# Spreading the mLSTM's stabiliser rows from POOL's queue, with the mask and the exponentials placed later

## The chip, the core and the metric

The kernel runs on one core of one Trainium2 chip. A core has TensorE (PE: matrix products and transposes into PSUM; PEld are its weight loads), VectorE (DVE), ScalarE (ACT: copies, activations), GpSimd (POOL: element-wise work in SBUF) and SyncE (SP), which in this kernel only issues transfers between HBM and SBUF. Sixteen DMA engines carry the transfers. Each engine runs its own program in order; where one needs another's result it waits on a semaphore. The metric is the device time of one execution in microseconds; less is better.

## What is computed

One layer of a decoder trunk over 2048 positions of width 1024, in float32: modulation and RMS norm, one combined projection, three mixers beside each other (forgetting attention, an mLSTM with matrix memory, a gated spatial unit), an output projection with residual, and a convolutional feed-forward part with residual. The change lies in the mLSTM. The reference, for one of its chunks:

```python
bcum = jnp.cumsum(fb, axis=-1)
log_d = bcum[..., :, None] - bcum[..., None, :] + ib[..., None, :]
log_d = jnp.where(causal, log_d, -jnp.inf)
log_inter = bcum + m[..., None]
m_t = jnp.maximum(log_inter, jnp.max(log_d, axis=-1))
w_intra = jnp.exp(log_d - m_t[..., None])
...
sc = jnp.einsum('bhtd,bhsd->bhts', qb, kb) * w_intra
num = (w_inter[..., None] * jnp.einsum('bhtd,bhde->bhte', qb, C)
       + jnp.einsum('bhts,bhse->bhte', sc, vb))
h_out = num / jnp.maximum(jnp.abs(den), jnp.exp(-m_t))[..., None]
```

The kernel takes chunks of 128 positions instead of 64; the result is the same. It holds w_intra transposed (keys in partitions, queries along the row), as exp(a_s + ne_t + mask): a_s is a column per head (`acol`), ne_t a row per head that every partition needs, and the mask is 0 or -1e30.

## The kernel before

**The stages.** The combined projection runs first, with attention after it, then the output projection, then the feed-forward part. The projection goes through the positions in two halves of 1024, and in each half through twelve blocks of up to 272 columns of W_in (lines 936 to 947). A block in natural order (`natural`, line 583) computes eight tiles `acc` of 128 positions, each of 24 matmuls (three float32r products over eight blocks of rows, `mm3`). `acc` has three PSUM buffers. What a block does with a tile differs: the blocks of k and q (`use_qk`, line 691) square it on ACT (`ev`, line 694), sum on DVE, take the inverse root on POOL (`ss`, the power instruction in `rsqrt`, line 132) and multiply on DVE (`qn`, line 700), which frees the tile; some steps later the tile is transposed (`turn`, line 703), evicted by ACT and DVE (`qhi`, `qlo`) and written to HBM. Blocks of v are evicted by ACT and DVE (`vhl`); the blocks of the spatial unit use ACT's Gelu (`ev`, line 640, `su`, line 658) and POOL (line 646 and the power instruction of `mu`).

**The mLSTM beside it.** `mlstm(qi)` (line 769) is a generator for 512 positions, four chunks of 128. Two of them are put into `background` behind block 3 of each half (line 982). After a tile's matmuls, `tick` (line 578) advances the first generator by one step, four times out of seven. A step is what lies between two yields.

- The first step computes the scans on DVE and writes `ne`, four rows of 512, to `ne_d` in HBM (line 799).
- Two yields later the columns (`ecol`, `acol`, `dcol`) are made and q, k, v are loaded (lines 803 to 826).
- `raw(n)` (line 830) transposes the keys of chunk n (PSUM tag `mp`, one buffer, also used by `spatial`, line 662, and by the modulation, line 461), copies them to `kT` on ACT (line 836), loads `M1` (line 838) and adds the mask to it on POOL (line 839). The load reads four rows of 128 values and spreads them over 128 partitions: 256 KB in pieces of 512 bytes. `M1` has two buffers.
- `decay(n)` (line 842) takes the four exponentials on ACT in place.
- Chunk n has two steps. In the first, scores and inter-chunk products go into PSUM; DVE multiplies the scores by M1 (`sc`, line 868), which is the last use of that M1, and makes `tm`. `decay(n+1)` is behind that. In the second step come the products with v, `H`, the weighted keys `kw` on POOL (line 884), the state update on DVE (line 898), and `raw(n+2)`.

**What sets the order.** Every transfer is issued by SP, with `dma = nc.sync.dma_start`. The source does not fix the order of an engine's program: a scheduler of the framework places each instruction by when it expects the inputs, a free buffer and the engine; source order ranks what is ready together. Once it is placed, an engine's program is run in order. The framework adds the waits; a transfer into a buffer waits on the issuing engine for the last reader.

Of the kernel before, what the change touches and what calls it, by code (L numbers as in the profile page):

```python
# [8 lines left out]
F32 = mybir.dt.float32  # L9
# [3 lines left out]
ALU = mybir.AluOpType  # L13
# [4 lines left out]
P = 128  # L18
# [15 lines left out]
def trunk(  # L34
# [7 lines left out]
    V, A, G, T = nc.vector, nc.scalar, nc.gpsimd, nc.tensor  # L42
    dma = nc.sync.dma_start
# [3 lines left out]
    def bc(ap, axis, n):  # L47
        u = ap.unsqueeze(axis)
        shape = list(u.shape)
        shape[axis] = n  # L50
        return u.broadcast_to(shape)
# [14 lines left out]
    ne_d = dr.tile([4, S], F32, name="ne_d")  # L66
# [62 lines left out]
    pool, pp = Mem(), Mem(PSUM)  # L129
# [219 lines left out]
    def down_open_right():  # L349
# [14 lines left out]
        ("R", 2048, 1), ("mprev", 20, 2), ("decr", 16, 2), ("ecol", 1088, 2), ("acol", 64, 2), ("dcol", 32, 2),  # L364
        ("qT", 4096, 1), ("kn", 4096, 1), ("v1", 4160, 1), ("H", 4160, 1), ("kT", 1024, 2), ("M1", 2048, 2),
        ("sc", 2048, 2), ("tm", 1040, 1), ("kw", 1024, 2), ("den", 64, 2), ("nd", 64, 2), ("mss", 64, 2),
# [12 lines left out]
    def misc_ps():  # L379
        return pp.tile([P, 512], F32, name="mp", tag="mp")  # L380

    def mps():
        return pp.tile([P, 512], F32, name="mps", tag="mps")
# [365 lines left out]
    maskT = pool.tile([P, P], F32, name="maskT")  # L749
# [19 lines left out]
    def mlstm(qi):  # L769
        t0 = qi * 512  # L770
# [56 lines left out]

        got = {}

        def raw(n):  # L830

            kps = misc_ps()
            for j in range(2):
                T.transpose(kps[:, j * P : (j + 1) * P], kn[:, n, j * P : (j + 1) * P], ident)
            kT = pool.tile([P, 2, P], F32, name="kT", tag="kT")
            A.copy(kT.rearrange("p a b -> p (a b)"), kps[:, 0:256])
            M1 = pool.tile([P, 4, P], F32, name="M1", tag="M1")
            dma(M1, ne_d[:, t0 + n * P : t0 + n * P + P].unsqueeze(0).broadcast_to([P, 4, P]))
            G.tensor_tensor(M1, M1, bc(maskT, 1, 4), op=ALU.add)
            got[n] = kT, M1  # L840

        def decay(n):
            M1 = got[n][1]
            for h in range(4):
                A.activation(M1[:, h, :], M1[:, h, :], AF.Exp, bias=acol[:, n, h : h + 1])

        yield
        raw(0)
        yield
        decay(0)  # L850
        raw(1)
        yield
        for n in range(4):
            ch = slice(n * P, n * P + P)
            kT, M1 = got.pop(n)

            sc = pool.tile([P, 4, P], F32, name="sc", tag="sc")
            tm = pool.tile([P, 4, 65], F32, name="tm", tag="tm")
            for par in range(2):
                hp = slice(par * 64, par * 64 + 64)  # L860
                eo = mps()
                for j in range(2):
                    T.matmul(eo[:, j * P : (j + 1) * P], kT[hp, j, :], qT[hp, j, ch], start=True, stop=True)
                for j in range(2):
                    T.matmul(
                        eo[:, 256 + j * 65 : 321 + j * 65], qT[hp, j, ch], Cst[hp, j, :], start=True, stop=True
                    )
                V.tensor_tensor(
                    sc[:, par::2, :], eo[:, 0:256].rearrange("p (j t) -> p j t", j=2), M1[:, par::2, :], op=ALU.mult
                )  # L870
                V.tensor_tensor(
                    tm[:, par::2, :], eo[:, 256:386].rearrange("p (j e) -> p j e", j=2),
                    bc(ecol[:, n, par:4:2], 2, 65), op=ALU.mult,
                )
            if n < 3:
                decay(n + 1)
            yield
            nps = mps()
            for h in range(4):
                T.matmul(nps[:, h * 65 : h * 65 + 65], sc[:, h, :], v1[:, n, h, :], start=True, stop=True)  # L880
            V.tensor_tensor(H[:, n], nps[:, 0:260].rearrange("p (h e) -> p h e", h=4), tm, op=ALU.add)

            kw = pool.tile([P, 4, 64], F32, name="kw", tag="kw")
            G.tensor_tensor(
                kw, kn[:, n, :].rearrange("p (h d) -> p h d", h=4), bc(ecol[:, n, 64:68], 2, 64), op=ALU.mult
            )
            ups = mps()
            for pr in range(2):
                T.matmul(
                    ups[:, pr * 130 : pr * 130 + 130],  # L890
                    kw[:, 2 * pr : 2 * pr + 2, :].rearrange("p h d -> p (h d)"),
                    v1[:, n, 2 * pr : 2 * pr + 2, :].rearrange("p h e -> p (h e)"),
                    start=True, stop=True,
                )
            for h in range(4):
                pr, hf = h // 2, h % 2
                hp = slice(hf * 64, hf * 64 + 64)
                V.scalar_tensor_tensor(
                    Cst[hp, pr, :], Cst[hp, pr, :], dcol[hp, pr, n : n + 1],
                    ups[hp, pr * 130 + hf * 65 : pr * 130 + hf * 65 + 65], op0=ALU.mult, op1=ALU.add,  # L900
                )
            if n < 2:
                raw(n + 2)
            yield

        den = pool.tile([P, 4, 4], F32, name="den", tag="den")
# [46 lines left out]
    for n, (half, i) in enumerate(steps):  # L953
# [27 lines left out]
        if i == 3:  # L981
            background += [mlstm(half * 2), mlstm(half * 2 + 1)]
# [633 lines left out]
```

## Time and profile before

| | |
|---|---|
| median of 3 runs | 2719.57 us (2718.58 to 2720.32) |
| profiled execution | 2712.34 us, its span 2710.6 us |
| mean granted TensorE clock | 0.985 |
| stage with the mLSTM, 150 to 760 us: TensorE busy | 551.35 of 610 us |
| ACT busy, POOL busy in that stage | 220.05 us, 149.31 us |
| power instruction of `ss` on POOL | 56 in that stage, mean 1126 ns |

A row of waits reads "who <- whom: us in total, times, longest". A row of the timeline is the start from the beginning of the span, the duration, the engine, the line, operation, the tiles written and read, and in brackets the idle time of the engine before it and what ended it. In rows of groups, three durations divided by strokes are the least, the median and the greatest in ns. M1 is called M in the profile, since buffer numbers are left out. Lines are those of the kernel above.

### The profile page before, as it was taken

How to read it: one execution, taken by the hardware profiler on the slowest of the kernel's cores; microseconds unless marked ns; L12 is line 12 of the kernel's file. 1: busy time of each engine (PE TensorE's matmuls, PEld its weight loads, DVE VectorE, ACT ScalarE, POOL GpSimd, SP SyncE). 2: the span in 40 equal slices, each digit the busy share in tenths (PEclk: the TensorE clock that was granted, in tenths of full speed). 3: DMA queues.
4: the chain of work that ended last, by engine and by line, in shares of the span. 5: the costliest groups of instructions: out<-in, count | busy, mean ns of one | idle time of the engine just before them, and what ended most of it. 6: DMA issues, size and time to landing. Idle time of an engine off the chain costs nothing.

```text
span 2710.6 us, 40295 instructions
## 1 busy us (share of the span) xinstructions
PE 2586.7 (95%) x14345; PEld 2218.3 (82%) x14345; DVE 2005.5 (74%) x3499; ACT 1305.0 (48%) x2452; POOL 453.4 (17%) x592
## 2 busy tenths in 40 slices
PE   6989899989899999999998999999999999999999
PEld 5988788989897877777786888888888888888787
DVE  7455466245457888885659988887988887898797
ACT  4243235243237887884436544444444444444443
POOL 2022222032335665651000000000000000000000
PEclk9989999999999999999999999999999999999999
DMA  7534465324356454525752322227222225849533
GB/s 251 170 89 145 120 186 178 108 52 148 92 144 170 110 142 117 166 63 190 263 206 70 103 82 87 78 86 287 94 85 80 86 79 180 293 135 312 172 104 117
DMA packets 313085, 382.09 MB, mean 141 GB/s; under 512 B 31004, under 2 KB 214264, under 8 KB 310836
## 3 DMA queue, kind: packets, MB, share of 16 engines
q1 hardware_dynamic: 312884, 379.52, 44.3%
q8 instruction: 113, 1.85, 0.3%
q14 instruction: 88, 0.72, 0.1%
HBM read 278.67 MB, written 100.77 MB: 140 GB/s over the span
## 4 chain that ended last, share of the span: by engine, by line
PE 57%; DVE 5%; ACT 2%; DMA 2%; issue 2%; POOL 1%; SPq 0%; DVEq 0%; ACTq 0%; POOLq 0%
PE ub L56 10%; PE ub L54 10%; PE ub L55 10%; PE db L55 4%; PE db L56 4%; PE db L54 4%; PE tp L263 3%; PE sp L210 3%; PE op L249 2%; PE wps L56 2%; PE wps L55 2%; PE wps L54 2%; PE op L250 2%; DVE wspl L1360 1%; ACT L L227 1%
## 5 line engine op out<-in xcount | busy, mean ns | idle before, releaser
L54 PE MATMUL acc<-whi,hh 128*128 128x256 f32 (+1 forms) x1408 | 419.6, 299 | 27.8 <-DVE qn L700 16.9
L56 PE MATMUL acc<-whi,hl 128*128 128x256 f32 (+1 forms) x1408 | 408.7, 292 | 0.1
L55 PE MATMUL acc<-wlo,hh 128*128 128x256 f32 (+1 forms) x1408 | 408.4, 291 | 0.0
L54 PEld LDWEIGHTS acc<-whi,hh 128*128 128x128 f32 x1408 | 278.9, 198 | 34.3 <-ACT ev L694 9.2
L54 PE MATMUL ub<-T,wsph 128*128 128x512 f32 x704 | 274.2, 390 | 5.8 <-ACT wsph L1228 5.8
L55 PEld LDWEIGHTS acc<-wlo,hh 128*128 128x128 f32 x1408 | 278.9, 198 | 0.5 <-issue 0.2
L56 PEld LDWEIGHTS acc<-whi,hl 128*128 128x128 f32 x1408 | 277.8, 198 | 1.0 <-DVE hl L548 0.7
L56 PE MATMUL ub<-T,wspl 128*128 128x512 f32 x704 | 273.7, 389 | 0.4 <-DVE wspl L1229 0.4
L55 PE MATMUL ub<-T,wsph 128*128 128x512 f32 x704 | 273.9, 389 | 0.0
L55 PE MATMUL db<-wspl,wsph 128*128 128x512 f32 x616 | 240.3, 390 | 2.7 <-DVE wspl L1360 2.7
L56 PE MATMUL db<-wsph,wspl 128*128 128x512 f32 x616 | 239.6, 389 | 0.0
L54 PE MATMUL db<-wsph 128*128 128x512 f32 x616 | 238.3, 389 | 0.3 <-ACT wsph L1359 0.3
L1228 ACT CAST wsph<-S 128x512 fp32r<-128x512 f32 x176 | 109.6, 623 | 229.4 <-PE ub L55 164.1
L267 DVE TENSOR_TENSOR plo<-tp,phi 128x512 fp32r<-128x512 f32 (+1 forms) x320 | 187.1, 607 | 34.2 <-ACT phi L266 32.0
L54 PE MATMUL ub<-B,wsph 128*128 128x512 f32 x528 | 207.2, 392 | 2.8 <-ACT wsph L1228 2.8
L56 PE MATMUL ub<-B,wspl 128*128 128x512 f32 x528 | 207.0, 392 | 0.7 <-DVE wspl L1229 0.7
L55 PE MATMUL ub<-B,wsph 128*128 128x512 f32 x528 | 207.1, 392 | 0.0
L227 ACT ACTIVATE L<-L,nm 128x1024 f32<-128x1024 f32 (+2 forms) x192 | 172.4, 902 | 33.0 <-DVE nm L216 30.3
L263 PE MATMUL tp<-ident,L 128*128 128x128 f32 x1088 | 179.6, 277 | 3.9 <-POOL L L232 1.2
L266 ACT CAST phi<-tp 128x512 fp32r<-128x512 f32 (+1 forms) x320 | 160.6, 521 | 44.2 <-PE tp L263 42.9
L210 PE MATMUL sp<-kk,q 128*128 128x512 f32 (+3 forms) x640 | 169.1, 375 | 2.6 <-DVE nm L216 1.6
L232 POOL TENSOR_SCALAR L<-L,rs 128x1024 f32<-128x1024 f32 (+2 forms) x192 | 167.3, 881 | 11.2
(334 smaller groups left out, 5897.5 us busy)
## 6 DMA issues: line engine op xcount, KB each, us to landing
w<-in_w_up_dram SPq DMA_DIRECT2D x88, 512.0 KB
wd<-in_w_down_dram SPq DMA_DIRECT2D x176, 256.0 KB
wa<-in_w_ada_dram SPq DMA_DIRECT2D x96, 256.0 KB
wst<-in_w_in_dram SPq DMA_DIRECT2D x48, 512.0 KB
act_d<-yc SPq DMA_DIRECT2D x44, 512.0 KB
act<-act_d SPq DMA_DIRECT2D x44, 512.0 KB
q<-q_d SPq DMA_DIRECT2D x128, 128.0 KB
hc_d<-hl SPq DMA_DIRECT2D x28, 512.0 KB
```

The lines of the kernel that those rows point to most:

```text
L54: T.matmul(ps, lh, rh, start=start, stop=False, skip_group_check=resume)
L55: T.matmul(ps, lh, rl, start=False, stop=False, skip_group_check=resume)
L56: T.matmul(ps, ll, rh, start=False, stop=stop, skip_group_check=resume)
L210: T.matmul(sp[:, b : b + bw], q2[n][:, qs], kk[:, s0 + b : s0 + b + bw], start=n == 0, stop=n == 1 and not last)
L227: A.activation(L[c], L[c], AF.Exp, bias=nm[:, n - 1 : n], scale=-1.0, accum_out=rs[:, c : c + 1])
L232: G.tensor_scalar(t, t, rs[:, 0:1], 1.0, op0=ALU.mult, op1=ALU.mult)
L249: T.matmul(op[:, c0:], vv[:, j, :], hi[:, c0:], start=(j == 0), stop=False)
L250: T.matmul(op[:, c0:], vv[:, j, :], lo[:, c0:], start=False, stop=(j == ns - 1))
L263: T.transpose(tp[:, i * P : (i + 1) * P], rows[i][j // 8][:, (j % 8) * P : (j % 8 + 1) * P], ident)
L266: A.copy(hi[:, c0:], tp[:, c0:])
L267: V.tensor_tensor(lo[:, c0:], tp[:, c0:], hi[:, c0:].bitcast(F32), op=ALU.subtract)
L1228: A.copy(hi, src)
```

## The change

`raw` is split in three: `spread` loads M1, `turned` transposes and copies the keys, `mask` adds the mask. The load is issued by POOL (`G.dma_start`) instead of SP. Spreads 0 and 1 stand in the step that loads q, k and v. Mask 0 stands a step later, mask 1 and the exponentials of chunk 0 two steps later. For the other chunks the spread stays at the end of chunk n's second step, the mask moves to the start of the next step, and the exponentials from the first to the second step of the chunk before the one that uses them. The amount of work, the tiles and their numbers of buffers are the same.

```diff
-        def raw(n):
+        def spread(n):
+
+            M1 = pool.tile([P, 4, P], F32, name="M1", tag="M1")
+            G.dma_start(M1, ne_d[:, t0 + n * P : t0 + n * P + P].unsqueeze(0).broadcast_to([P, 4, P]))
+            got["M", n] = M1
+
+        def turned(n):
 
             kps = misc_ps()
             for j in range(2):
                 T.transpose(kps[:, j * P : (j + 1) * P], kn[:, n, j * P : (j + 1) * P], ident)
             kT = pool.tile([P, 2, P], F32, name="kT", tag="kT")
             A.copy(kT.rearrange("p a b -> p (a b)"), kps[:, 0:256])
-            M1 = pool.tile([P, 4, P], F32, name="M1", tag="M1")
-            dma(M1, ne_d[:, t0 + n * P : t0 + n * P + P].unsqueeze(0).broadcast_to([P, 4, P]))
-            G.tensor_tensor(M1, M1, bc(maskT, 1, 4), op=ALU.add)
-            got[n] = kT, M1
+            got["k", n] = kT
+
+        def mask(n):
+            G.tensor_tensor(got["M", n], got["M", n], bc(maskT, 1, 4), op=ALU.add)
 
         def decay(n):
-            M1 = got[n][1]
+            M1 = got["M", n]
             for h in range(4):
                 A.activation(M1[:, h, :], M1[:, h, :], AF.Exp, bias=acol[:, n, h : h + 1])
 
+        spread(0)
+        spread(1)
         yield
-        raw(0)
+        mask(0)
+        turned(0)
         yield
+        mask(1)
         decay(0)
-        raw(1)
+        turned(1)
         yield
         for n in range(4):
             ch = slice(n * P, n * P + P)
-            kT, M1 = got.pop(n)
+            kT, M1 = got["k", n], got["M", n]
+            if 1 <= n < 3:
+                mask(n + 1)
...
-            if n < 3:
-                decay(n + 1)
             yield
             nps = mps()
...
             if n < 2:
-                raw(n + 2)
+                spread(n + 2)
+                turned(n + 2)
+            if n < 3:
+                decay(n + 1)
             yield
```

## The prediction

> **What bounds the kernel now.** I read the page first, then the stage in which the mLSTM runs (150 to 760 us), then that stage's waits engine by engine, then two of its stalls in the timeline.
>
> ```profile
> span 2710.6 us, 40295 instructions
> PE 2586.7 (95%) x14345; PEld 2218.3 (82%) x14345; DVE 2005.5 (74%) x3499; ACT 1305.0 (48%) x2452; POOL 453.4 (17%) x592
> q1 hardware_dynamic: 312884, 379.52, 44.3%
> ```
> ```profile
> core 0: us, PE busy (x) PEld busy (x) DVE busy (x) ACT busy (x) POOL busy (x), PEclk, DMA share, GB/s
> 150.00:760.00 610.00, 551.35 (x4224) 529.31 (x4223) 322.87 (x780) 220.05 (x422) 149.31 (x142) 0.95 0.43 123
> ```
>
> TensorE carries the span, so a change on other engines is worth what it takes off TensorE's idle time. In this stage TensorE is busy 551.35 of 610 us: 58.7 us idle. Its granted clock is 0.95, so 610 x 0.05 = 30 us are lost to half-clock stretches that follow such stalls. All data transfers go through one queue, q1; none is issued by POOL. TensorE's waits in the stage, the eight rows that matter here:
>
> ```profile
> PE acc L54 <- DVE qn L700: 16.9, 9, 8.4
> PE mp L668 <- ACT kT L836: 7.3, 2, 4.0
> PE acc L54 <- ACT ev L640: 6.3, 4, 2.2
> PE mp L834 <- DVE sh L474: 4.7, 1, 4.7
> PE trp L706 <- DVE qlo L711: 4.5, 1, 4.5
> PE mps L863 <- DVE H L881: 2.5, 1, 2.5
> PE acc L54 <- ACT ev L694: 2.2, 1, 2.2
> PE acc L54 <- ACT su L658: 1.1, 1, 1.1
> ```
>
> They sum to 45.5 us. None names M1 (M in the profile). What stands behind them is one level down, in the waits of POOL, ACT and SP:
>
> ```profile
> POOL M L839 <- DMA M<-ne_d: 102.7, 15, 27.0
> ACT M L845 <- POOL M L839: 65.7, 13, 8.6
> SPq L838 <- DVE sc L868: 48.2, 7, 26.3
> ```
>
> POOL waits for M1's rows to land, ACT waits for POOL's mask, and what both engines have behind those instructions (the inverse root of q and k on POOL, evictions of acc on ACT) comes late to TensorE. One such case, in the timeline of SP, POOL, ACT and PE (start, us, engine, line):
>
> ```profile
> 328.27 0.37 SPq L838 DMA_DIRECT2D M<-ne_d  x1
> 328.68 0.50 SPq L414 DMA_DIRECT2D wa<-in_w_ada_dram  x1
> ```
> ```profile
> 337.39 1.26 POOL L839 TENSOR_TENSOR M<-M,maskT 128x512 f32<-128x512 f32 x1 [8.39 <-DMA M<-ne_d]
> ```
> ```profile
> 338.69 1.28 ACT L845 ACTIVATE M<-M,acol 128x128 f32<-128x128 f32 x4 [8.63 <-POOL M L839]
> 339.87 0.36 ACT L694 ACTIVATE ev<-acc 128x256 f32<-128x256 f32 x1
> ```
> ```profile
> 341.23 0.66 PE L706 MATMUL trp<-ident,qn 128*128 128x128 f32 x2 [4.54 <-DVE qlo L711]
> ```
>
> The transfer is issued at 328.27 and the mask starts at 337.39: 9 us for 256 KB. ACT stands still 8.63 us with an eviction (ev L694) behind the exponentials; TensorE loses 4.54 us. Followed back in the same manner, the stalls of these eight rows that are over 1 us end nearly all in a late M1. The ceiling of any cure is 45.5 us of idle time and its share of the lost clock: 30 x 45.5 / 58.7 x 551 / 610 = 21 us, together 66 us. A stalled microsecond thus counts 1.46.
>
> **Whether the steps in the source are steps in the engines.** The programs of the engines are not in source order. raw(0) and raw(1) stand in two steps, yet their transfers go out together, and exponentials that stand behind sc in the source run before it:
>
> ```profile
> 297.18 0.98 SPq L838 DMA_DIRECT2D M<-ne_d  x2
> ```
> ```profile
> 349.85 0.42 DVE L868 TENSOR_TENSOR sc<-mps,M 128x256 f32<-128x256 f32 x1
> ```
>
> The four exponentials at 338.69 are decay(2), in the source behind sc of chunk 1 at 349.85. So a scheduler places each instruction where it expects its inputs, source order deciding only between instructions that are expected at one time. It expected the landing sooner than the 9 us it took, for it put mask and exponentials ahead of evictions that could have run. Moving a line by a step therefore does not buy a step; it buys lower rank in a tie.
>
> **The change, part by part.** The rows of M1's instructions, and what one DMA looks like while it is alone:
>
> ```profile
> L845 ACT ACTIVATE M<-M,acol x64: 385/387/405, 172.0 to 736.1; 128x128 f32<-128x128 f32 x64
> L838 SPq DMA_DIRECT2D M<-ne_d x16: 359/378/638, 162.5 to 726.1; - x16
> L839 POOL TENSOR_TENSOR M<-M,maskT x16: 1260/1272/1295, 170.7 to 733.9; 128x512 f32<-128x512 f32 x16
> ```
> ```profile
> DMA packets 410, 0.21 MB, mean 36 GB/s; under 512 B 0, under 2 KB 410, under 8 KB 410
> ```
>
> (1) The kT copy now ranks ahead of the exponentials, since turned(n+2) stands before decay(n+1). It was the other way round, and this view of ACT and PE shows the price:
>
> ```profile
> 226.43 0.99 ACT L845 ACTIVATE M<-M,acol 128x128 f32<-128x128 f32 x3 [7.46 <-POOL M L839]
> 229.01 0.37 ACT L836 COPY kT<-mp 128x256 f32<-128x256 f32 x1
> ```
> ```profile
> 229.43 0.70 PE L668 MATMUL mp<-sv,wT 128*128 128x256 f32 x2 [4.00 <-ACT kT L836]
> ```
>
> Both stalls of the kT row, 7.3 us, come to 7.3 x 1.46 = 10.7 us. Bounds 0 and 10.7; I take half, 5 us, since a tie must exist for rank to matter.
>
> (2) The exponentials (64 x 0.387 us, no more and no fewer) rank behind the evictions of one more step. The rows that an eviction ahead of them would relieve are ev L640, ev L694, su, sh, qlo and H: 21.3 us, 31 us with the clock. Bounds 0 and 31. The four take 1.28 us; a tile of acc comes about every 3 us, as POOL's instruction for each shows:
>
> ```profile
> 321.35 1.01 POOL L132 TENSOR_TENSOR ss<-ss,nhalf 128x4 f32<-128x4 f32 x1 [2.22 <-DVE ss L697]
> 324.43 1.01 POOL L132 TENSOR_TENSOR ss<-ss,nhalf 128x4 f32<-128x4 f32 x1 [2.08 <-DVE ss L697]
> ```
>
> So a tie is had in somewhat under half the cases; I take a third of the price, 10 us.
>
> (3) The mask (1.27 us on POOL) ranks behind the ss instructions of a step. The row is qn, 16.9 us, 25 us with the clock. The largest piece, 8.4 us, is two masks in a row and stays. Bounds 0 and 25; I take a quarter, 6 us. Covering all of these is the landing; if it comes later still, (1) to (3) shrink, not grow.
>
> (4) SP loses 16 issues of 0.378 us and its waits for a free M1 (48.2 us over 7). In the 5.8 us from 329.2 to 335.0 only M1's 410 packets of 512 bytes moved, while the wa transfer issued at 328.68 stood in the same queue. Who waited for such transfers:
>
> ```profile
> DVE modacc L424 <- DMA wa<-in_w_ada_dram: 21.8, 8, 7.8
> ```
>
> No row of TensorE names that transfer; bounds 0 and a tenth of 21.8; I take 2 us. The Trainium skill speaks against even this: "DMA: Bandwidth & Descriptors", section "SWDGE vs HWDGE vs iDMA" (Issuing engines are not separate DMA queues), has transfers of all issuers on the same 16 engines and only issue time saved; by it this term is 0 and the sum is smaller by 2 us.
>
> (5) POOL gains 16 issues. Nothing in the trace shows one. The least is SP's 0.378 us; the most is that POOL makes each packet at the pace they flow, 5.8 / 410 x 512 = 7.2 us. I take 1.3 us, the row of POOL that walks the same 512 columns, the mask. All 16 are 21 us, on an engine busy 149.31 of 610, so as busy time they are hidden; if POOL were full they would cost 21. What is not hidden is that each landing comes 1.3 - 0.4 = 0.9 us later, at the 13 places where ACT waits: 12 us lost. Bounds: 0 and 16 x 3.4 = 54 (below).
> The Trainium skill, "DMA: Bandwidth & Descriptors", section "Specifications", gives about 1 us to the first byte of a POOL-issued transfer and 0.6 to one of SP's; by that the term would be 13 x 0.4 = 5 us, an estimate that no row here can confirm.
>
> A wait is also moved: POOL, not SP, now waits for sc to free an M1. Behind it on POOL stand kw, mu and ss, for which DVE and then TensorE wait. The scheduler puts the issue behind the expected sc, so I take it at nothing; its other bound is the 48.2 us of SP's row, of which SP's running ahead is a part.
>
> Sum: -5 - 10 - 6 - 2 + 12 = -11 us. The profiled execution took 2712.34 us (span 2710.6 and 1.74 around it), 7 us under the median of 2719.57; the difference carries over: 2701 for such an execution, 2709 for the median.
>
> **The rivals.** *Nothing moves.* The scheduler puts transfers, masks and exponentials where they were, and the landing takes the same 9 us. For it: the hoisting shown above, and M1's own pace. 36 GB/s is slow against the stage's mean of 123, so the slowness lies in the transfer, not in its queue. Time 2720.
>
> *POOL is held by its own transfers (slower).* POOL runs in order, and writing 512 packets, or waiting for sc before it may, keeps ss behind it. Place: the k and q blocks, where each acc tile needs one ss. Price: the present waits average 102.7 / 15 = 6.8 us and cost TensorE 45.5 / 15 = 3.0, so some 3.8 us of a hold are covered. It decides from a hold of 3.8 us: at 5.5 us it adds 16 x 1.7 = 27 us, time 2746; at 7.2 us 54. Against it: the mask's 1.27 us for as many columns. The Trainium skill, "SBUF — State Buffer", section "SBUF: two separate sides" (the DVE blocks DMA trap), adds that some VectorE operations lock POOL out of writing its descriptors; no row of this trace can show it.
>
> *The waits go.* If the scheduler expects POOL's transfers to land late, it places masks and exponentials behind enough work, and 40 of the 66 us or more are won: 2680 and below. For it speaks only that a 9 us landing is hidden by three tiles of 3 us; against it, that nothing tells the scheduler.
>
> **How the numbers follow.** The forecast has 0.36, with a range of its own of 2695 to 2714: terms (1) to (4) whole or nearly nothing. Waits gone 0.07, nothing moves 0.22, POOL held 0.35. Measurement tells about 0.2% (5.4 us) from no change, so faster is 0.36 + 0.07 = 0.43, same 0.22, slower 0.35. The range 2680 to 2746 leaves out the waits-gone case (0.07) and the upper end of POOL's hold (about 0.1).
>
> **What would show it.** Right: the mask's wait for the transfer stays near 100 us in all, ACT's wait for the mask falls below 65.7, the kT row of TensorE (7.3) is gone, and a POOL issue takes 1 to 2 us. Wrong: POOL's issue over 3.8 us with qn's row above 16.9 (POOL held); or mask and exponential waits near nothing and a stage clock near 1.00 (waits gone); or eight rows that still sum to 45 (nothing moved).

## The result, and the profile after

| | before | after |
|---|---|---|
| median | 2719.07 us (2716.41 to 2720.32, 4 runs) | 2740.09 us (2738.02 to 2741.53, 4 runs) |
| profiled execution, its span | 2712.34, 2710.6 us | 2741.53, 2739.8 us |
| mean granted clock | 0.985 | 0.981 |

The ratio is 1.0078, with an interval of 1.0061 to 1.0095: slower by 21 us. The forecast was faster by 11. In the two traces after is 21.4 us late when the projection ends, at 808.8 us of before, and all of that arises beside the mLSTM; the spans differ by 29, since before's profiled execution lies 7 us under its median.

The queues, in the page of after: POOL's transfers have a queue of their own now, q0, with the 4.20 MB of M1.

```profile
q1 hardware_dynamic: 304436, 375.32, 43.2%
q0 software_dynamic: 1280, 4.20, 2.6%
```

M1's transfer in the view of its tile, then the two rows of waits that were to fall (lines of after: spread 833, mask 846, exponentials 851, kT 842):

```profile
L833 POOL DMA_DIRECT2D M<-ne_d x16: 747/814/988, 163.9 to 745.6; - x16
...
DMA to landing us min/median/max: 8.2/9.3/15.2
```
```profile
POOL M L846 <- DMA M<-ne_d: 96.5, 16, 9.5
ACT M L851 <- POOL M L846: 76.3, 12, 11.0
```

An issue holds POOL for 0.81 us, less than forecast. The transfer takes some 9 us from either queue: where no other M1 is ahead of it, the mask starts 7.8 to 9.5 us after the issue in before, and 8.3 to 11.0 us after. ACT waits more for the mask, 76.3 against 65.7 us. TensorE's rows and its stage:

```profile
PE acc L54 <- DVE qn L700: 18.1, 8, 10.9
PE acc L54 <- ACT ev L694: 9.1, 1, 9.1
PE acc L54 <- ACT ev L640: 8.9, 3, 6.6
PE mp L668 <- ACT kT L842: 8.0, 2, 4.7
PE mp L840 <- DVE sh L474: 5.7, 1, 5.7
PE acc L54 <- ACT kT L842: 4.7, 1, 4.7
PE mps L875 <- DVE H L891: 4.3, 1, 4.3
```
```profile
150.00:760.00 610.00, 529.56 (x4038) 508.49 (x4036) 309.39 (x742) 221.46 (x415) 154.44 (x153) 0.94 0.49 121
```

TensorE is busy 21.8 us less in the same 610 us. The row of qn as a whole hardly grew (18.1 against 16.9), but other waits stand in it: the 9.1 us of ev L694 come at the place where qn cost 8.4 before. The longest new wait is qn's 10.94 us, and POOL's timeline tells what made it; first after, then the same place before:

```profile
692.32 1.56 POOL L833 DMA_DIRECT2D M<-ne_d  x2 [17.37 <-ACT ev L694]
694.13 1.02 POOL L132 TENSOR_TENSOR ss<-ss,nhalf 128x4 f32<-128x4 f32 x1 [0.24 <-DVE ss L697]
703.34 1.26 POOL L846 TENSOR_TENSOR M<-M,maskT 128x512 f32<-128x512 f32 x1 [8.19 <-DMA M<-ne_d]
708.46 1.26 POOL L846 TENSOR_TENSOR M<-M,maskT 128x512 f32<-128x512 f32 x1 [3.86 <-DMA M<-ne_d]
709.67 1.18 POOL L894 TENSOR_TENSOR kw<-kn,ecol 128x256 f32<-128x256 f32 x2
710.81 1.01 POOL L132 TENSOR_TENSOR ss<-ss,nhalf 128x4 f32<-128x4 f32 x1
```
```profile
683.53 1.01 POOL L132 TENSOR_TENSOR ss<-ss,nhalf 128x4 f32<-128x4 f32 x1 [19.17 <-DVE ss L697]
684.72 0.61 POOL L884 TENSOR_TENSOR kw<-kn,ecol 128x256 f32<-128x256 f32 x1 [0.18 <-ACT ecol L808]
691.22 1.26 POOL L839 TENSOR_TENSOR M<-M,maskT 128x512 f32<-128x512 f32 x1 [5.89 <-DMA M<-ne_d]
692.44 1.01 POOL L132 TENSOR_TENSOR ss<-ss,nhalf 128x4 f32<-128x4 f32 x1
693.42 0.61 POOL L884 TENSOR_TENSOR kw<-kn,ecol 128x256 f32<-128x256 f32 x1
695.48 1.28 POOL L839 TENSOR_TENSOR M<-M,maskT 128x512 f32<-128x512 f32 x1 [1.44 <-DMA M<-ne_d]
```

Before, ss runs between the masks and waits for one transfer. After, the same ss stands behind both masks and waits for two. The changed source lines are not the reason: e1_queue below has before's source with POOL's issue, and there too ss stands behind both masks. The scheduler ordered POOL's instructions anew when it had to place POOL's issues among them. The 17.37 us in the first row are no new cost, though: POOL stood still 19.17 us there before, under another name. POOL's wait for the tile's release (`tm`, 9.5 us over 3 in the waits of after) is small too.

### The profile page after: what moved, and what is told of

The parts are those of the page before. It is cut to its first block, busy times and chain, and to the rows that moved or that the text cites. A ratio compares the mean times of both kernels' runs of the same rounds, so it can differ in the third digit from the quotient of the medians.

```text
span 2739.8 us, 40300 instructions
## 1 busy us (share of the span) xinstructions
PE 2589.2 (95%) x14345; PEld 2220.8 (81%) x14345; DVE 2005.1 (73%) x3499; ACT 1312.3 (48%) x2458; POOL 464.6 (17%) x608
## 4 chain that ended last, share of the span: by engine, by line
PE 49%; DVE 6%; DMA 3%; ACT 1%; issue 1%; POOL 1%; SPq 0%; DVEq 0%; ACTq 0%; POOLq 0%
PE ub L56 10%; PE ub L55 10%; PE ub L54 10%; PE db L55 4%; PE db L56 4%; PE db L54 4%; PE wps L55 1%; PE wps L56 1%; PE wps L54 1%; DVE wspl L1373 1%; PE tp L263 1%; PE sp L210 1%; DMA wd<-in_w_down_dram 1%; DMA ld<-y_d 1%; PE op L249 1%
## 5 line engine op out<-in xcount | busy, mean ns | idle before, releaser
L54 PE MATMUL acc<-whi,hh 128*128 128x256 f32 (+1 forms) x1408 | 420.3, 299 | 43.7 <-DVE qn L700 18.1
```

Source lines behind the costliest of these rows:

```text
L54: T.matmul(ps, lh, rh, start=start, stop=False, skip_group_check=resume)
```

## The experiments

Each run's "before" is measured with it; its medians lie between 2718.4 and 2721.2 us. In the code cuts, `ne_d[...]` shortens the source of the load (the columns `t0 + n * P` to `t0 + n * P + P`, spread over the partitions), and a line of `...` stands for lines left out. In the runs with a loop of loads or a fill, the lines below it have numbers one higher than in before.

**Which part of the change costs.** The queue alone, in before's kernel:

```diff
-            dma(M1, ne_d[...])
+            G.dma_start(M1, ne_d[...])
```

> The kernel before, with only the issue of M1's load moved from SP to POOL; order of source lines as before. Theory A (POOL's queue costs it: later issue, longer landing, one more instruction of 0.81 us ahead of the inverse roots): all of the +21 us is here, 2735 to 2745. Theory B (the other places that mask, key copy and exponentials get in the engines' orders cost it): near the kernel before, 2714 to 2726. Theory C (each some): 2728 to 2733.

2741.37 us, ratio 1.0081 [1.0066, 1.0096]. The change with its load given back to SP:

```diff
-            G.dma_start(M1, ne_d[...])
+            dma(M1, ne_d[...])
```

> The kernel after, with M1's load issued by SP again; the order of source lines as after. Theory A (POOL's queue): near the kernel before, 2714 to 2726. Theory B (order): all of the +21 us is here, 2735 to 2745. Theory C (each some): 2726 to 2732. If order and queue add up, this and the run with the queue alone together show +21 us.

2719.49 us, ratio 0.9997 [0.9986, 1.0008]. So the queue, with what the scheduler makes of it, is the whole loss, and the new order of the source is worth nothing: ACT's wait for the mask is 64.5 us in this run, before it was 65.7. The traces show why. On POOL no mask has moved behind an ss; the program is that of before but for two kw. On ACT some 20 of 2406 instructions stand elsewhere, exponentials behind evictions among them. Two runs bound what could be had; first no load at all (the exponentials then lack the term of the rows):

```diff
-            dma(M1, ne_d[...])
-            G.tensor_tensor(M1, M1, bc(maskT, 1, 4), op=ALU.add)
+            G.tensor_tensor(M1, bc(maskT, 1, 4), bc(maskT, 1, 4), op=ALU.add)
```

> The kernel before without M1's load: the mask is written to M1 by POOL from the mask tile alone, so the row term of the exponentials is left out. Write of the rows to HBM, POOL's instruction and the exponentials stay. If the landing of M1 is what stands behind TensorE's stalls in the mLSTM stage, as the prediction has it, 40 to 66 us go: 2655 to 2680, and the key copies no longer hold TensorE. If other waits take their place: 2690 to 2710. If the landing never bound: 2715 to 2723.

2666.15 us, ratio 0.9803 [0.9788, 0.9818]: the load is worth 54 us, under the ceiling of 66, and the row of the key copies falls from 7.3 to 1.4 us. And the rows written 16 times, so that 16 partitions each read their own (the rows of a copy are also 8704 bytes apart, for 8192 in before):

```diff
-    ne_d = dr.tile([4, S], F32, name="ne_d")
+    ne_d = dr.tile([16, 4, S + P], F32, name="ne_d")
...
-        dma(ne_d[:, t0 : t0 + 512], ne)
+        dma(ne_d[:, :, t0 : t0 + 512].rearrange("c h t -> h c t"), bc(ne, 1, 16))
...
-            dma(M1, ne_d[...])
+            for g in range(8):
+                dma(M1[g * 16 : g * 16 + 16], ne_d[:, :, t0 + n * P : t0 + n * P + P])
```

> The kernel before with the rows written to HBM in 16 copies and M1 loaded by eight transfers of 16 partitions, each partition from a copy of its own, all from SP. Theory D (the landing takes 9 us because all 16 DMA engines read the same few lines of HBM): M1 lands in 3 to 5 us after the first issue, the mask's waits fall from 103 us to under 50 us, the time to 2680 to 2700. Theory E (it is slow for its pieces of 512 bytes, or for the load's form): landing still 8 us or more, time 2719 or, for eight issues instead of one, up to 2735.

2684.55 us, ratio 0.9871 [0.9854, 0.9889]. A gain of 36 us, as expected; that it is due to the lines read does not follow, since the load is also split (below) and the rows stand otherwise.

**What the queue costs by.** A fill of M1 on POOL ahead of SP's transfer, as a stand-in for the hold:

```diff
+            G.memset(M1, 0.0)
             dma(M1, ne_d[...])
```

> Before's kernel, SP's issue kept; POOL fills the free M1 with zeros (128x512, by the 128x128 fill of 0.20 us some 0.8 us, the length of POOL's issue) and the transfer waits for that fill. So POOL is taken for as long, and waits in its order for the same free buffer, as when it issues the transfer itself; the transfer stays on q1. Theory P (the 21 us are POOL's: an instruction of 0.8 us which waits for the old sc and which ss, ev and the mask stand behind, and the transfer starts after it): 2732 to 2744 us. Theory Q (they are the queue's: the transfer lands later from POOL's own queue): 2718 to 2725 us.

2719.18 us, ratio 1.0001 [0.9992, 1.001]. The fill took 0.525 us, not 0.8, and needs no rows in HBM, so the scheduler put those of a block's first two chunks early; for the other two it does what POOL's issue does, waits for sc (28.3 us over 7) and holds ss. That was free. ACT's queue instead:

```diff
-            dma(M1, ne_d[...])
+            A.dma_start(M1, ne_d[...])
```

> Before's kernel with M1's transfer issued from ACT's queue, so on neither SP's queue nor POOL's; POOL's instructions are those of before. Theory P: ACT, the busier engine, now holds the issue and waits for the free M1, so 2720 to 2740 us with ACT's waits for sc in the trace, and landing as in before (8 to 9.3 us single). Theory Q: landing grows as on POOL's queue (9.3 in the middle, up to 15 us), 2732 to 2745 us.

2730.1 us, ratio 1.0038 [1.0026, 1.005]. Inside theory P's band, with the mask 7.9 to 9.8 us after the issue, as in before; yet inconclusive, for the scheduler moved masks and exponentials in this kernel too. 64 copies, by 2 loads of 64 partitions from SP, and then from POOL (diff as for 16 copies, with the numbers changed):

> The rows written to DRAM in 64 copies, and M1 loaded from SP by 2 transfers of 64 partitions, each partition from its own copy; otherwise before's kernel. With 16 copies and 8 transfers the run took 2684.55 us with 9.4 us of POOL's waits left. If only the reads of one line cost: 2680 to 2687 us, as with 16 copies. If SP's 128 issues of 0.59 us cost too: 2668 to 2680 us. If the larger write (512 KB a block) shows: 2688 to 2700 us.

> The same 64 copies and 2 transfers, issued from POOL's queue: 32 POOL issues in place of 16. Theory P (POOL's time and its order cost, whatever the landing): 15 to 40 us above f3_c64. Theory Q or a cost that hangs on the slow landing (masks and what stands behind them late): 0 to 6 us above f3_c64.

2697.88 us, ratio 0.9924 [0.991, 0.9937], and 2717.19, ratio 0.9991 [0.9982, 1.0001]. POOL's queue, with the scheduler free, costs 19 us again, though its loads now land 3.0 us after the issue in the middle. So the cost does not hang on the slow landing. With theory P weakened by the fill and theory Q by this, the order of POOL's instructions remained as a suspect, and it can be tested by itself. In e1_queue TensorE's program is that of before but for one swap of neighbours, and of POOL's 588 computing instructions 19 stand in another place. Chained by explicit edges of order, each of the two orders can be had with each of the two queues:

```diff
         trunk(tc, *args)
...
+        ins = [i for i in nc.cur_bb.bb.instructions if i.engine == mybir.EngineType.Pool and type(i).__name__ in ops]
...
+        for a, b in zip(order, order[1:]):
+            tc.add_manual_dep(ins[b], ins[a].name, behind, reason="order")
```

> Before's kernel with SP issuing, but with POOL's computing instructions chained in the order in which the scheduler put them when POOL issued the transfer (19 of 588 stand elsewhere: the two masks of a block ahead of ev or ss that stood before them); PE's order is that of before. Theory R (the cost is the order of POOL's instructions, which the scheduler changed when it had to place the issue among them): 2734 to 2743 us. Theory S (the cost is the transfer's own: issue later by 0.3 to 0.7 us, landing later by 0.4 to 3 us): 2716 to 2724 us.

> The reverse: POOL issues the transfer, and POOL's computing instructions are chained in before's order. Theory R: 2717 to 2726 us. Theory S: 2734 to 2743 us. If each is half of it: both runs near 2730 us.

| | POOL in before's order | POOL in e1_queue's order |
|---|---|---|
| SP issues | 1 (before) | 1.0029 [1.0017, 1.0041] |
| POOL issues | 1.0036 [1.0024, 1.0048] | 1.0081 [1.0066, 1.0096] |

Neither theory alone, and nearest to the third line, each about half: the order costs 7 us, the transfer from POOL's queue 9, together 16 of the 21 (the intervals leave room for the rest). Only POOL was chained, so the split is not quite clean: in g2_pool_placed 12 of VectorE's instructions stand elsewhere than in before, much the same as in e1_queue, and in e1_queue five of ACT's besides. About half of VectorE's moves are in f1_hold too, which lost nothing; the moves on ACT were not tried by themselves. POOL's timeline of g1_sp_placed shows the order at work with SP issuing, ss behind both masks:

```profile
699.06 1.26 POOL L839 TENSOR_TENSOR M<-M,maskT 128x512 f32<-128x512 f32 x1 [7.17 <-DMA M<-ne_d]
702.94 1.26 POOL L839 TENSOR_TENSOR M<-M,maskT 128x512 f32<-128x512 f32 x1 [2.62 <-DMA M<-ne_d]
704.16 1.18 POOL L884 TENSOR_TENSOR kw<-kn,ecol 128x256 f32<-128x256 f32 x2
705.30 1.01 POOL L132 TENSOR_TENSOR ss<-ss,nhalf 128x4 f32<-128x4 f32 x1
```

For the other part, POOL issues half of the transfers, in before's order, first those of a block's first two chunks, then those of the others:

```diff
-            dma(M1, ne_d[...])
+            (G if n < 2 else nc.sync).dma_start(M1, ne_d[...])
```

> POOL's computing instructions chained in before's order; POOL issues only the transfers of the first two steps of each block (8 of 16, which wait for the rows to reach DRAM), SP the other 8. With all 16 from POOL in this order: 2729.67 us, some 9 above before. Theory T (the cost is in the pairs: two issues in a row hold mu, ev and ss behind them, and the second lands up to 15 us later): 2726 to 2732 us. Theory U (it is in the steps, where the transfer waits for sc and starts 0.3 to 0.7 us later): 2718 to 2723 us.

> The reverse: POOL issues the transfers of the third and fourth steps (8 of 16), SP those of the first two; before's order of POOL's computing. Theory T: 2718 to 2723 us. Theory U: 2726 to 2732 us. If the cost is spread: both near 2725 us.

2722.25 us, ratio 1.0008 [1.0, 1.0017], and 2724.84, ratio 1.0016 [1.0005, 1.0027]. The first lies inside theory U's line, the second in no line but nearest to "spread". Together they make 8 of the 9 us, but their intervals overlap, and that of the first touches none, so these runs do not tell where the cost sits.

**Making the load quick.** 16 copies with the change's order of the source, and 32 copies by 4 loads of 32 partitions in before's:

> 16 copies of the rows with 8 loads of 16 partitions from SP, together with the change's order of steps (mask and exponentials each a step behind). With 16 copies and before's order: 2684.55 us, of which 9.4 us of POOL's waits for the transfer are left. If the order pays once landing is quick: 2668 to 2680 us; if it is worth nothing: 2680 to 2690 us.

> 32 copies, 4 loads of 32 partitions from SP, before's order. Between 16 copies (2684.55 us) and 64 (2697.88 us): if the larger write (64 copies: 512 KB a block) costs, about 2689 us; if SP's 128 issues cost, 2675 to 2683 us.

2682.82 us, ratio 0.9863 [0.9845, 0.988], and 2665.62, ratio 0.9797 [0.9781, 0.9812]. The order of the source is worth nothing again. 32 copies are the fastest version, 55 us under before, level with no load at all. That is under both lines of the record, while 64 copies fell under "the larger write shows". From the write of the rows to the first load the second block of 512 positions takes 1.4 us with one copy, 7.2 with 16, 13.3 with 32 and 23.8 with 64. The waits and the stage (150 to 800 us; before: 590.82 and 0.95) of g4_c32:

```profile
POOL M L840 <- DMA M<-ne_d: 13.2, 9, 5.8
ACT M L846 <- POOL M L840: 11.4, 7, 3.1
```
```profile
150.00:800.00 650.00, 615.85 (x4811) 585.43 (x4809) 383.14 (x905) 235.80 (x496) 188.03 (x196) 0.99 0.49 143
```

Then the change's order and POOL's queue with 32 copies:

> 32 copies and 4 loads from SP, with the change's order of steps. With before's order: 2665.62 us, no more than without any load (2666.15 us). If the load no longer ends any wait that counts, the order is worth nothing: 2662 to 2670 us. If it has a cost of its own which the slow landing hid: above 2672 us.

> 32 copies and 4 loads, issued from POOL's queue, before's order of steps. 64 issues of 0.6 us on POOL. With 64 copies the queue cost 19 us over SP. If the queue's cost is its place on POOL: 2680 to 2695 us. If it needs the slow landing: 2664 to 2672 us.

2670.18 us, ratio 0.9819 [0.9806, 0.9832], and 2680.37, ratio 0.9864 [0.985, 0.9878]. The order of the source is 5 us slower if anything, between the two lines of the record; POOL's queue costs 15, with 64 issues of 0.55 us and a landing of 2.7. Three versions pay 15 to 21 us for it whether POOL issues 16, 32 or 64 times.

**Is it the copies or the split?** The rows written once, the load split in four:

```diff
-            dma(M1, ne_d[...])
+            for g in range(4):
+                dma(M1[g * 32 : g * 32 + 32], ne_d[...].unsqueeze(0).broadcast_to([32, 4, P]))
```

> The rows written once, as in before, but M1 loaded by 4 transfers of 32 partitions from SP, as with the 32 copies (2665.62 us). Theory D (many partitions reading the same lines make the load slow): no gain, 2715 to 2735 us, with the wait of POOL's mask for the transfer still near 100 us. Rival (one transfer of 128 partitions is slow and four smaller ones are not, whatever they read): 2662 to 2675 us, that wait near 13 us.

2686.11 us, ratio 0.9872 [0.9854, 0.9889]. Neither line of the record foresaw this: 35 us won with a landing as slow as before. Theory D was right about the landing and wrong about the time. With all four issues within 1.75 us, from 194.10 on, the mask waits for the rows until 203.22; over the run, loads with no M1 ahead and their issues close together need 7.8 to 10.1 us from the first issue to the mask that waits for them. Yet POOL's and ACT's waits fell, from 102.7 and 65.7 us:

```profile
POOL M L840 <- DMA M<-ne_d: 48.3, 10, 16.5
ACT M L846 <- POOL M L840: 30.5, 8, 7.9
```

SP, POOL and ACT, where before had lost 8.63 us (here the second two of the four transfers are issued 2.9 us after the first two):

```profile
319.83 0.80 SPq L839 DMA_DIRECT2D M<-ne_d  x2
```
```profile
328.87 1.38 POOL L840 TENSOR_TENSOR M<-M,maskT 128x512 f32<-128x512 f32 x1 [0.33 <-DMA q_d<-qhi]
```
```profile
324.24 0.38 ACT L694 ACTIVATE ev<-acc 128x256 f32<-128x256 f32 x1 [2.67 <-PE acc L56]
325.13 0.37 ACT L836 COPY kT<-mp 128x256 f32<-128x256 f32 x1 [0.51 <-PE mp L834]
...
326.79 1.05 ACT L569 CAST whi<-wst 128x1024 fp32r<-128x1024 f32 x1 [0.81 <-PE acc L56]
330.28 0.40 ACT L846 ACTIVATE M<-M,acol 128x128 f32<-128x128 f32 x1 [2.44 <-POOL M L840]
```

The scheduler has placed an eviction, the keys' copy and a cast ahead of the exponentials, which in before stood behind them, and all of that runs while the load lands; the wait is 2.44 us. On POOL kw and one more ss or ev stand ahead of most masks. That the order won the 35 us follows from the landing being the same; this order with a single load was not run. The last run has the quick load in before's order of POOL's and ACT's instructions (32 copies, both engines chained as above):

> 32 copies and 4 loads from SP, with POOL's and ACT's computing instructions chained in before's order through the mLSTM stage, so that only the transfers differ from before. The split alone (i1) took 35 us off although the mask still starts some 8 to 10 us after the first issue: there the scheduler had put more work ahead of the mask. If quick landing by itself is worth the rest only (55 - 35): 2695 to 2705 us. If quick landing is worth all of it in any order: 2663 to 2675 us. If the first load's wait for the larger write eats it in this order: 2710 us or more.

2714.24 us, ratio 0.9983 [0.9974, 0.9991]. The third line of the record holds. TensorE's and VectorE's programs were left free, and some 100 of VectorE's instructions stand elsewhere than in before, so not only the transfers differ. POOL's wait for the rows is in all what it was (102.7 us before):

```profile
POOL M L840 <- DMA M<-ne_d: 101.2, 13, 34.1
```

It is made up otherwise. In before's order both masks of a block stand ahead of all that POOL has to do meanwhile, and the first waits for the copies to be written: ahead of the first masks of the four blocks POOL stands idle 63.6 us together, 37.3 in before; ahead of the other twelve 44.8, 75.6 in before. So 4 us is not the price of a quick landing alone, but what is left of it when the larger write is paid. A quick landing without the larger write was not run. POOL, then TensorE, in i2_c32_placed:

```profile
311.06 1.26 POOL L840 TENSOR_TENSOR M<-M,maskT 128x512 f32<-128x512 f32 x1 [34.10 <-DMA M<-ne_d]
313.86 1.26 POOL L840 TENSOR_TENSOR M<-M,maskT 128x512 f32<-128x512 f32 x1 [1.54 <-DMA M<-ne_d]
315.08 1.18 POOL L885 TENSOR_TENSOR kw<-kn,ecol 128x256 f32<-128x256 f32 x2
316.22 1.01 POOL L132 TENSOR_TENSOR ss<-ss,nhalf 128x4 f32<-128x4 f32 x1
```
```profile
317.84 0.55 PE L54 MATMUL acc<-whi,hh 128*128 128x256 f32 x1 [13.23 <-DVE qn L700]
```

In g4_c32, at the same place, the scheduler had put both kw and three ss ahead of the first mask, and POOL stood idle 5.80 us for it, not 34.10. With the same transfers, the two runs are 49 us apart: that is the order's, of all the engines' programs.

## Why the prediction was wrong

- **What bounds the kernel** held: taking the load away, or hiding it, gave 54 and 55 us of a ceiling put at 66, and the stage clock went to 0.99. Which lever moves it was read wrongly.
- **Terms (1) to (3), -21 us, failed.** The step was that a lower rank in the source pays in "a third" or "a quarter" of the cases. With SP's queue the order gave -1 us, with an interval on both sides of none, -2 us with 16 copies and +5 with 32. The prediction had said itself that the scheduler places by when it expects inputs, with source order for ties only. The third rested on how often the trace has two instructions close together (1.28 us in every 3), which is not how often the scheduler sees a tie; the half and the quarter had no row behind them. In e2_order no mask moved behind an ss at all, and the exponentials that moved won nothing. Here the rival *nothing moves* was right.
- **Term (4), -2 us**, shows in no run: each run that gives the 16 issues to another engine loses by it, 9 us in g2_pool_placed and 10 in f2_actq. The Trainium skill, "DMA: Bandwidth & Descriptors", section "SWDGE vs HWDGE vs iDMA", says that transfers of all issuers run on the same 16 engines and that only issue time is saved, by which the term is 0; the landing of 9 us from q0 as from q1 agrees.
- **Term (5), +12 us**, measured 9 in before's order (g2_pool_placed). The size is near: from the end of the sc that frees M1 to the mask, the eight later loads took 9.2 us on average in before and 10.0 in g2_pool_placed, 0.8 us more where 0.9 was forecast. The parts are not: an issue takes 0.81 us, not 1.3. On POOL it mostly starts 0.30 to 0.78 us after that sc, where SP's mostly starts 0.06 to 0.09 after, and from issue to mask it is 9.3 us in the middle, not 8.8. These 9 us were not taken apart further by a run that could tell.
- **The step that turned the sign** besides (1) to (3): the issue's place on POOL was taken "at nothing", since the scheduler would put it behind the expected sc. It did, and in doing so placed masks ahead of ss and ev: 7 us (g1_sp_placed). In sum, about 0 for the -21, none for the -2, 9 for the 12 and 7 for the nothing give 16 of the 21 us measured; the cause of the other 5 stays open.
- The rival *POOL is held by its own transfers* came nearest in time, 2746, by luck: its reason does not hold, for it needed a hold of 3.8 us, and the issue takes 0.81. Loss by ss kept late on POOL was its place, and that was right (qn, 10.94 us), though masks kept it late and not the issue.
- The rival *the waits go* was given 0.07 because "nothing tells the scheduler" that the load lands late. True of this change, and it is the lever: in i1_split, with four issues in place of one, the scheduler put masks and exponentials behind more work, and 35 us were won with the same landing. That it expected the load later is inferred from this order; no trace shows what it expects.
- Of the signs named, the mask's wait near 100 us came (96.5); ACT's wait rose, the kT row stayed (8.0), and the issue was shorter than 1 us. Of the sign for POOL held, half came: qn's row above 16.9 (18.1), without the hold.

## What to carry to other kernels

Where a scheduler writes the engines' programs, compare those programs before and after an edit, instruction by instruction: here 19 moved instructions on POOL cost 7 us where a gain of 11 was intended, and moved source lines gained nothing. A late load costs by what stands behind its first reader: with the landing as slow as ever, another order won 35 us, and with the quick landing the order made 49 us of difference. So try first to put work ahead of the reader. To price a queue, run the queue and the order of instructions separately, for moving an issue to a computing engine changes both.

## What the hardware showed that was not expected

- POOL's issue of a transfer of 128 partitions, four rows of 512 bytes each, held it 0.75 to 0.99 us; for 64 partitions 0.62, for 32 partitions 0.55. Four times the pieces take half as long again.
- M1's load, when no other M1 is ahead of it, takes 8 to 11 us from the issue to the mask while one copy of the rows is read, by one transfer or by four, from SP, ACT or POOL. With 32 copies and the same four transfers (595.17 to 599.51 us in i2_c32_placed) it takes 4.3 us, of which the four issues are 2.5. Bytes, pieces and the number of transfers are the same in i1_split; the lines read differ, and with them the distance of the rows (8704 bytes, not 8192), which no run separates. So it is likely, but not shown alone, that many readers of the same lines make the load slow; why was not tried.
